# A hybrid decoder step on one core: the fourth gate-and-up tile in seven block products

## The chip, the core and the metric

The kernel runs on one core of a Trainium2 chip. A core has five engines that each work through their own queue in order: TensorE (PE: matmuls, with the weight load beside it, PEld), VectorE (DVE), ScalarE (ACT), GpSimd (POOL) and SyncE (SP), which here only issues transfers. Engines wait for each other by semaphores. Matmul results go to PSUM, which has eight banks; everything else lies in SBUF. The metric is the device time of one execution in microseconds, the median of several runs. The profile shows one further execution.

## The reference

One step of a decoder layer for 520 tokens: 512 of a prompt and 8 samples, which share the weights. Model width 1024. The layer has a recurrent branch and an attention branch, and then the part that the change touches, a SwiGLU feed-forward layer of width 2816:

```python
h2 = rms_norm(x, norm2_g) * (1.0 + sc2) + sh2
gu, up = jnp.split(h2 @ w_ffn_in, 2, axis=-1)
x = x + g2 * ((jax.nn.silu(gu) * up) @ w_ffn_out)
```

All data are float32.

## The kernel before

Activations lie transposed: 128 features on the partitions, 520 tokens along the free axis, worked in two halves of 260 tokens, left (L) and right (R). To keep float32 accuracy with the faster float32r matmul, every operand is split into a high and a low part: ScalarE casts the high part ("whi", "wb", "tuh"), VectorE subtracts it for the low part ("wlo", second half of "wb", "tul"). Every product is three matmuls: high by high, low weight by high, high weight by low.

The feed-forward layer goes over 22 tiles of 128 columns, each with a gate and an up part. Tiles 0 and 1 are done plainly by halves (groups "fi", lines 1654 to 1679), tiles 2 and 3 plainly by `ffn_tile` ("fig" and "fiu", two products of 48 matmuls each): 96 matmuls of 260 tokens for a tile. From tile 4 (`GROUP`) on, `fast_tile` uses a Winograd form of Strassen's scheme. The 2 x 2 blocks are gate and up by the two halves of the 1024 features for the weights (a11, a12, a21, a22), and the halves of features by the halves of tokens for the input. Seven block products of 12 matmuls (four chunks of 128 features, three matmuls each) take the place of eight: 84 matmuls. For them POOL forms four sums of the weights of each tile (s1 to s4, lines 261 to 264, tile "ws"), and once for all tiles the sums u and w of the input (`h2_blocks`, lines 1593 to 1600; each has a left and a right part, for four chunks k). The sums are split into high and low parts by `split_blocks` ("tu" and "tw"). The seven products add up in four banks X, Y, W, Z; VectorE combines these (line 1617), ScalarE takes the silu of the gate, and `close` multiplies and splits a half of the tile's output for the second matrix.

The products with the second matrix ("fo") are strewn between the blocks of later tiles (`JOIN`): the group of tiles 0 to 3 is multiplied during tiles 4 to 7, the first of them after block S2 of tile 4.

Order. `begin` runs before each product: it loads weights that are due within 22 us and splits those due within 11 us, by an estimated length of each unit (5.36 us for a plain product, 1.34 us for a block). `units` lists the products in order. The weight sums of a tile are issued when its first block, A11, is split. Raw weights of a tile have two buffers ("wraw"), split weights three of each of two tags ("whi", "wlo"), and seven buffers of the tag "pg" hold h2 before its split, the weight sums and the second matrix's raw weights. Instructions traced in this order go to a planner, which makes the order on each engine from it: what is ready by its own estimate may go ahead of what is not. `issue_after` holds a block of instructions behind a given one; `split_blocks` stands behind the silu that was traced last. `defer(k, ...)` runs a function after the k-th product from now: the sums of chunks 0 and 1 are split after tile 2's gate product, those of chunks 2 and 3 after its up product.

Of the kernel before, what the change touches and what calls it, by code (L numbers as in the profile page):

```python
# [11 lines left out]
AF = mybir.ActivationFunctionType  # L12
ALU = mybir.AluOpType
# [10 lines left out]
FF = 2816  # L24
# [4 lines left out]
HALF = NT // 2  # L29
# [36 lines left out]
def kernel(ctx, tc, xT, par, gates, b_f, cst, cse, own, cache_k, cache_v, cache_lf, pt,  # L66
# [3 lines left out]
    pe, act, dve, pool, sp = nc.tensor, nc.scalar, nc.vector, nc.gpsimd, nc.sync  # L70
# [46 lines left out]
    def cols(src, c0, n=256, k0=0, nk=KT):  # L117
        return [(src, k0, nk, c0, n)]
# [21 lines left out]
    GROUP = 4  # L140
    PLAIN = 2
    LAST = 16
    JOIN = {}
    for jt in range(GROUP, LAST):
        JOIN[jt] = {"S2": (jt // GROUP - 1, 2 * (jt % GROUP)), "A12": (jt // GROUP - 1, 2 * (jt % GROUP) + 1)}
    for i, (jt, name) in enumerate(((16, "S2"), (16, "A12"), (17, "A12"), (18, "A12"), (19, "A12"), (20, "A12"),
                                    (21, "S2"), (21, "A12"))):
        JOIN.setdefault(jt, {})[name] = (LAST // GROUP - 1, i)
    BLOCKS = ("A11", "S2", "S3", "S1", "A12", "A22", "S4")
    units = []  # L150

    def whole(c):
        for o in range(0, sum(p[4] for p in chunks[c]), 128):
            units.append((c, o, chunks[c][0][2]))
# [4 lines left out]
    for jt in range(FF // 128):  # L159
        c = len(chunks)  # L160
        chunks.append(cols(w_fi, 128 * jt, 128) + cols(w_fi, FF + 128 * jt, 128))
        if jt < GROUP:
            whole(c)
            continue
        for name in BLOCKS:
            units.append((c, name, 4))
            if name in JOIN[jt]:
                g, i = JOIN[jt][name]
                if i % 2 == 0:
                    joined.add(len(chunks))  # L170
                    chunks.append(cols(w_fo, 128 * i, 256, 128 * GROUP * g, GROUP))
                units.append((max(joined), 128 * (i % 2), GROUP))
# [8 lines left out]
    state = {"n": 0, "dma": 0, "split": 0, "load": 22, "lead": 11, "due": 0, "age": 1}  # L181
# [73 lines left out]
    def split_block(raw, name):  # L255
        if name == "A11":
            a11, a12, a21, a22 = (raw[:, k:k + 4, o:o + 128] for o in (0, 128) for k in (0, 4))
            s12, s34 = (pgp.tile([128, 8, 128], F32, name="ws", tag="pg") for _ in range(2))
            s1, s2, s3, s4 = s12[:, :4], s12[:, 4:], s34[:, :4], s34[:, 4:]
            blocks.update(A11=a11, A12=a12, A22=a22, S1=s1, S2=s2, S3=s3, S4=s4)  # L260
            pool.tensor_tensor(s1, a21, a22, ALU.add)  # L261
            pool.tensor_tensor(s2, s1, a11, ALU.subtract)
            pool.tensor_tensor(s3, a11, a21, ALU.subtract)
            pool.tensor_tensor(s4, a12, s2, ALU.subtract)
        return split_four(blocks[name])

    def split_four(src):
        state["tag"] = "wlo" if state.get("tag") == "whi" else "whi"
        t = wp.tile([128, KT, 128], F32R, name="wb", tag=state["tag"], bufs=3)
        state["act"] = act.copy(t[:, :4], src)  # L270
        state["last"] = dve.tensor_tensor(t[:, 4:], src, t[:, :4].bitcast(F32), ALU.subtract)  # L271
        return [t[:, k] for k in range(4)], [t[:, 4 + k] for k in range(4)]
# [9 lines left out]
    def defer(k, fn):  # L282
        later.setdefault(state["n"] + k, []).append(fn)
# [50 lines left out]
    def split(name, raw, scale=None):  # L334
        hi = slot(name + "h", dt=F32R)
        lo = slot(name + "l", dt=F32R)
        if scale is None:
            act.copy(hi, raw)
            dve.tensor_tensor(lo, raw, hi.bitcast(F32), ALU.subtract)
        else:  # L340
            act.activation(hi, raw, AF.Copy, scale=scale)
            dve.scalar_tensor_tensor(lo, raw, scale, hi.bitcast(F32), ALU.mult, ALU.subtract)
        return hi, lo
# [551 lines left out]
    for i in range(KT):  # L895
        if i % 4 == 0:
            qtp.append(bank(f"qt{i}", NS))
        if i < 6:
            t = qpart[i]
            for j, (t0, t1) in enumerate(HALVES):  # L900
                b = bank(f"q{i}_{j}")
# [672 lines left out]
    def pair_out():  # L1574
        return slot("ach", dt=F32R), slot("acl", dt=F32R)

    def ffn_tile(jt):
        t, out = slot("sw"), pair_out()
        product(f"fig{jt}", h2, lambda j, b: swish(b, t, j))

        def up(j, b):
            t0, t1 = HALVES[j]
            times_up(b, t, j)
            split_part(out, t[:, t0:t1], slice(t0, t1))

        product(f"fiu{jt}", h2, up)
        return out


    L_, R_ = slice(0, HALF), slice(HALF, NT)  # L1590
    tb, traw = [], []
# [7 lines left out]
        pool.tensor_tensor(u[:, R_], b2[:, L_], w[:, L_], ALU.subtract)  # L1599
        traw.append((u, w))  # L1600

    def split_blocks(k0):
        with tc.issue_after(state["silu"].ins):
            for k in range(k0, k0 + 2):
                u, w = traw[k]
                tb.append((split("tu", u), split("tw", w)))

    def h2_block(name, k):
        pair, part = {"A11": (h2[k], L_), "A12": (h2[k + 4], L_), "S4": (h2[k + 4], R_), "S1": (tb[k][0], L_),
# [3 lines left out]
    def fast_tile(jt, ac):  # L1613
        sw, cp, u2, out = slot("sw"), slot("cp"), slot("u2", HALF), pair_out()
        X, Y, W, Z = (bank(f"fi{jt}{n}")[:, :HALF] for n in "xywz")
        into = {"A11": X, "S2": Y, "S3": W, "S1": Z, "A12": X, "A22": W, "S4": Z}
        add = lambda o_, a_, b_: dve.tensor_tensor(o_, b_, a_, ALU.add)

        def close(b, part):
            dve.tensor_tensor(b, b, sw[:, part], ALU.mult)  # L1620
            split_part(out, b, part)

        for m_, name in enumerate(BLOCKS):
            n = begin()
            hi, lo = splits[n]
            for k in range(4):
                ah, al = h2_block(name, k)
                for m, (wt, at) in enumerate(((hi, ah), (lo, ah), (hi, al))):
                    state["mm"] = pe.matmul(into[name], lhsT=wt[k], rhs=at, start=m_ < 4 and k == 0 and m == 0,
                                            stop=k == 3 and m == 2, skip_group_check=m_ > 3)  # L1630
            if name == "A11":
                act.copy(cp[:, L_], X)
            elif name == "S2":
                add(u2, cp[:, L_], Y)
            elif name == "S3":
                add(W, u2, W)
            elif name == "S1":
                act.copy(cp[:, R_], Z)  # L1638
                add(Z, u2, Z)
                add(Y, cp[:, R_], W)  # L1640
            elif name == "A12":
                act.activation(sw[:, L_], X, AF.Silu)
            elif name == "A22":
                close(W, L_)
            elif name == "S4":
                act.activation(sw[:, R_], Z, AF.Silu)
                close(Y, R_)
            run_later(n)
            if name in JOIN[jt]:
                g, i = JOIN[jt][name]  # L1650
                product(f"fo{g}_{i}", ac[GROUP * g:GROUP * g + GROUP], lambda j, b_, i=i: residual(i, b_, 5, j))
        return out

    ac, ts, ready = [], [slot("sw") for _ in range(PLAIN)], []
    u = state["n"]
    for j in range(2):
        for m in range(2 * PLAIN):
            if j == 0:
                begin(u + 3)
            b = bank(f"fi{m}_{j}")  # L1660
# [10 lines left out]
            first = u + 2 * PLAIN  # L1671
# [8 lines left out]
    for jt in range(PLAIN, FF // 128):  # L1680
        if jt == PLAIN:
            for k in range(4):
                h2_blocks(k)
            defer(0, lambda: split_blocks(0))
            defer(1, lambda: split_blocks(2))
        ac.append(fast_tile(jt, ac) if jt >= GROUP else ffn_tile(jt))
    last_product(ac[LAST:])


# [60 lines left out]
```

## Time and profile before

| | us |
|---|---|
| median of 3 runs | 1027.86 (1024.04 to 1030.81) |
| profiled execution | 1027.04 |
| its span, first to last instruction | 1025.3 |
| TensorE busy | 994.1 (97%) |
| VectorE busy | 792.7 (77%) |
| ScalarE busy | 553.3 (54%) |
| POOL busy | 331.4 (32%) |

The mean granted clock of TensorE was 0.993 of full speed. In the rows of the profile a line number is that of the code above, then come engine, operation, and output<-inputs by the program's names, with shapes. In a timeline the first two numbers are start and length in us; a bracket gives the idle time of the engine before the instruction and what ended it. In the chain of work a row is start, length, engine and name. A row of the wait table gives who waited for whom: us in total, times, longest.

### The profile page before, as it was taken

To read this page: it belongs to the slowest core of one execution; us is meant where nothing else is said; L and a number is where in the kernel's file an instruction comes from. 1 tells how busy PE (TensorE), PEld (TensorE's weight loads), DVE (VectorE), ACT (ScalarE), POOL (GpSimd) and SP (SyncE) were. 2 spreads that over 40 slices of the span, in tenths; PEclk is the share of its full clock that TensorE was granted. 3 is DMA by queue.
4 is the path that set the end of the run, shared out by engine and by line. 5 is a ranking of instruction groups with operands and counts; after the bars stand their busy time and mean duration, and the time that the engine had idled before them with its cause. 6 is when DMAs were issued, how large, how long until landed. Compare 5 with 4: busy or idle time off the path is not lost.

```text
span 1025.3 us, 21277 instructions
## 1 busy us (share of the span) xinstructions
PE 994.1 (97%) x7994; PEld 921.1 (90%) x7994; DVE 792.7 (77%) x1423; ACT 553.3 (54%) x1132; POOL 331.4 (32%) x424
## 2 busy tenths in 40 slices
PE   4999999999999999999999999999999999999996
PEld 1888989999999988888888989999999999999996
DVE  5446999998999978887656554878888878888764
ACT  4433665857682267777875234464444444445453
POOL 0224511111135135454430001494442433434212
PEclk9899999999999999999999999999999999999999
DMA  9888987778899999997775784324243242333212
GB/s 324 308 278 292 306 284 222 261 232 276 266 277 322 322 324 292 287 311 219 235 236 190 252 295 114 83 63 122 64 124 105 82 124 78 88 104 104 63 63 84
DMA packets 164378, 206.98 MB, mean 202 GB/s; under 512 B 9890, under 2 KB 125106, under 8 KB 164210
## 3 DMA queue, kind: packets, MB, share of 16 engines
q1 hardware_dynamic: 147554, 152.52, 47.7%
q0 software_dynamic: 13040, 46.67, 13.9%
q10 hardware_dynamic: 3680, 6.42, 1.7%
q8 instruction: 63, 1.03, 0.4%
q14 instruction: 41, 0.34, 0.1%
HBM read 192.49 MB, written 13.09 MB: 201 GB/s over the span
## 4 chain that ended last, share of the span: by engine, by line
PE 86%; DVE 6%; DMA 4%; ACT 1%; issue 1%; POOL 1%; SPq 0%; DVEq 0%; ACTq 0%; POOLq 0%
PE fo L305 12%; PE gr L305 5%; PE gb L305 5%; PE pa L305 5%; PE pb L305 4%; PE v L305 4%; PE k L305 4%; PE ga L305 4%; PE xr L305 3%; PE pv L817 3%; PE wo L305 3%; DMA wraw<-in_w_in_dram 2%; PE qp L527 2%; PE po L1273 2%; PE q L527 1%; PE ptt L1239 1%
## 5 line engine op out<-in xcount | busy, mean ns | idle before, releaser
L246 ACT CAST whi<-wraw 128x1024 fp32r<-128x1024 f32 (+1 forms) x79 | 82.0, 1040 | 114.2 <-PE pb L305 35.1
L248 DVE TENSOR_TENSOR wlo<-wraw,whi 128x1024 fp32r<-128x1024 f32 (+1 forms) x79 | 100.4, 1272 | 22.9 <-ACT whi L246 20.1
L270 ACT CAST wb<-ws 128x512 fp32r<-128x512 f32 x72 | 44.7, 621 | 91.0 <-PE fo L305 63.6
L305 PE MATMUL fo<-ach,wb 128*128 128x260 f32 x512 | 93.3, 282 | 0.0
L682 POOL DMA_DIRECT2D pg<-in_cache_k_dram x74 | 39.5, 534 | 143.4 <-DVE S L731 77.0
L271 DVE TENSOR_TENSOR wb<-wraw,wb 128x512 fp32r<-128x512 f32 x86 | 74.3, 864 | 6.5 <-ACT wb L270 5.4
L305 PEld LDWEIGHTS fo<-ach,wb 128*128 128x128 f32 x512 | 78.9, 188 | 0.0
L261 POOL TENSOR_TENSOR ws<-wraw 128x512 f32<-128x512 f32 x18 | 26.1, 1449 | 153.6 <-DMA wraw<-in_w_fi_dram 121.1
L271 DVE TENSOR_TENSOR wb<-ws,wb 128x512 fp32r<-128x512 f32 x72 | 63.1, 876 | 15.3 <-ACT wb L270 13.4
L270 ACT CAST wb<-wraw 128x512 fp32r<-128x512 f32 x86 | 53.5, 622 | 37.7 <-ACT cp L1638 6.5
L305 PE MATMUL fo<-acl,wb 128*128 128x260 f32 x256 | 72.2, 282 | 0.0
L730 DVE TENSOR_TENSOR pg<-pg,qb 128x1024 f32<-128x1024 f32 x48 | 57.9, 1219 | 0.8 <-DMA pg<-in_cache_k_dram 0.8
L731 DVE TENSOR_REDUCE S<-pg 128x16 f32<-128x1024 f32 x48 | 57.4, 1209 | 0.3
L1230 POOL TENSOR_SCALAR p<-p,mu 128x128 f32<-128x128 f32 (+3 forms) x28 | 38.7, 1391 | 52.2 <-DVE mu L1226 38.1
L305 PEld LDWEIGHTS fo<-acl,wb 128*128 128x128 f32 x256 | 48.2, 188 | 0.0
L1224 ACT ACTIVATE p<-p,mu 128x128 f32<-128x128 f32 (+3 forms) x64 | 35.4, 554 | 18.7 <-DVE mu L1223 18.4
L305 PE MATMUL v<-hh,whi 128*128 128x260 f32 x128 | 37.9, 296 | 0.8 <-ACT row L797 0.5
L305 PE MATMUL pb<-oh,whi 128*128 128x260 f32 x128 | 36.8, 287 | 1.0 <-ACT oh L1331 1.0
L305 PE MATMUL k<-hh,whi 128*128 128x260 f32 x128 | 37.3, 291 | 0.0
L305 PE MATMUL gb<-hh,whi 128*128 128x260 f32 x128 | 37.0, 289 | 0.0
L305 PE MATMUL v<-hl,whi 128*128 128x260 f32 x128 | 37.0, 289 | 0.0
L305 PE MATMUL v<-hh,wlo 128*128 128x260 f32 x128 | 36.9, 288 | 0.0
(1099 smaller groups left out, 3968.6 us busy)
## 6 DMA issues: line engine op xcount, KB each, us to landing
araw<-in_ada_w_dram SPq DMA_DIRECT2D x48, 512.0 KB, 6.4
wraw<-in_w_fi_dram SPq DMA_DIRECT2D x44, 512.0 KB, 4.3
pg<-in_cache_k_dram POOLq DMA_DIRECT2D x42, 512.0 KB, 5.8
pg<-in_cache_v_dram SPq DMA_DIRECT2D x42, 512.0 KB, 5.4
wraw<-in_w_in_dram SPq DMA_DIRECT2D x34, 512.0 KB, 7.4
wraw<-in_w_in_dram SPq DMA_DIRECT2D x11, 1024.0 KB, 9.3
pg<-in_cache_v_dram POOLq DMA_DIRECT2D x22, 512.0 KB, 6.2
pg<-in_cache_k_dram POOLq DMA_DIRECT2D x32, 256.0 KB, 5.8
```

The costliest lines, as they stand in the source:

```text
L246: state["act"] = act.copy(hi[:, :k1 - k0], src)
L248: state["last"] = dve.tensor_tensor(lo[:, :k1 - k0], src, hi[:, :k1 - k0].bitcast(F32), ALU.subtract)
L270: state["act"] = act.copy(t[:, :4], src)
L271: state["last"] = dve.tensor_tensor(t[:, 4:], src, t[:, :4].bitcast(F32), ALU.subtract)
L305: state["mm"] = pe.matmul(out[:, :t1 - t0], lhsT=wt[k], rhs=at, start=k == 0 and m == 0, stop=k == nk - 1 and m == 2)
L527: state["mm"] = pe.matmul(b[:, :HALF], lhsT=wt, rhs=at[:, t0:t1], start=k == 0 and m == 0, stop=k == 3 and m == 2)
L682: done.append(eng.dma_start(pg, cache[bass.ds(r, 1), :, c0:c1].rearrange("a p c -> (a p) c")))
L730: dve.tensor_tensor(pg, pg, q, ALU.mult)
L731: last = dve.tensor_reduce(S[r // 2][:, c:c + H], pg.rearrange("p (h d) -> p h d", d=DH), AX.X, ALU.add)
L817: pe.matmul(pv[0][32 * gq:32 * gq + 32, :], lhsT=pw[r][:, c:c + 32], rhs=pgs[gq // 2][:, 512 * hf:512 * hf + 512], start=j == 0, stop=j == ...
L1224: act.activation(p[:, :n + 128], p[:, :n + 128], AF.Exp, bias=mu[:, 0:1], scale=-1.0, accum_out=mu[:, 1:2])
L1230: (pool.tensor_scalar(p, p, mu[:, 2:3], None, ALU.mult) if a and i + 1 < KT else act.activation(p, p, AF.Copy, scale=mu[:, 2:3]))
```

## The change

Tile 3 is computed by `fast_tile` too. Its blocks have an order of their own (A11, A12, S4, S2, S3, S1, A22 instead of A11, S2, S3, S1, A12, A22, S4). As S4 comes before the products that it is added to, it has a bank of its own ("v"), is copied to SBUF and added after S1; the right half of the output is closed after S1, the left half after A22. On POOL the tile's fourth weight sum is traced before the third. The input's sums are split in one go after tile 2's gate product: the four w, then the four u.

```diff
-    BLOCKS = ("A11", "S2", "S3", "S1", "A12", "A22", "S4")
+    BLOCKS = [("A11", "S2", "S3", "S1", "A12", "A22", "S4")] * (FF // 128)
+    FIRST = 3
+    BLOCKS[FIRST] = ("A11", "A12", "S4", "S2", "S3", "S1", "A22")
...
-        if jt < GROUP:
+        if jt < FIRST:
             whole(c)
             continue
-        for name in BLOCKS:
+        for name in BLOCKS[jt]:
...
             pool.tensor_tensor(s1, a21, a22, ALU.add)
             pool.tensor_tensor(s2, s1, a11, ALU.subtract)
+            if "V" not in state:
+                pool.tensor_tensor(s4, a12, s2, ALU.subtract)
             pool.tensor_tensor(s3, a11, a21, ALU.subtract)
-            pool.tensor_tensor(s4, a12, s2, ALU.subtract)
+            if "V" in state:
+                pool.tensor_tensor(s4, a12, s2, ALU.subtract)
+            state["V"] = 1
...
-    def split_blocks(k0):
+    def split_blocks():
         with tc.issue_after(state["silu"].ins):
-            for k in range(k0, k0 + 2):
-                u, w = traw[k]
-                tb.append((split("tu", u), split("tw", w)))
+            tw = [split("tw", w) for _, w in traw]
+            tb.extend(zip([split("tu", u) for u, _ in traw], tw))
...
+        first = jt == FIRST
+        if first:
+            into["S4"] = bank(f"fi{jt}v")[:, :HALF]
+            v = slot("v4", HALF)
...
                 add(Z, u2, Z)
                 add(Y, cp[:, R_], W)
+                if first:
+                    add(Z, v, Z)
+                    act.activation(sw[:, R_], Z, AF.Silu)
+                    close(Y, R_)
             elif name == "A12":
                 act.activation(sw[:, L_], X, AF.Silu)
             elif name == "A22":
                 close(W, L_)
+            elif name == "S4" and first:
+                act.copy(v, into[name])
...
-            defer(0, lambda: split_blocks(0))
-            defer(1, lambda: split_blocks(2))
-        ac.append(fast_tile(jt, ac) if jt >= GROUP else ffn_tile(jt))
+            defer(0, split_blocks)
+        ac.append(fast_tile(jt, ac) if jt >= FIRST else ffn_tile(jt))
```

In the matmuls, `start` is set for the first block in a bank instead of by the block's number.

More of the change, by code (lines that the diff above doesn't have):

```diff
@@ L161 @@
         chunks.append(cols(w_fi, 128 * jt, 128) + cols(w_fi, FF + 128 * jt, 128))
-        if jt < GROUP:
+        if jt < FIRST:
             whole(c)
             continue
-        for name in BLOCKS:
+        for name in BLOCKS[jt]:
             units.append((c, name, 4))
-            if name in JOIN[jt]:
+            if name in JOIN.get(jt, ()):
                 g, i = JOIN[jt][name]
@@ L1616, in fast_tile @@
         into = {"A11": X, "S2": Y, "S3": W, "S1": Z, "A12": X, "A22": W, "S4": Z}
+        first = jt == FIRST
+        if first:
+            into["S4"] = bank(f"fi{jt}v")[:, :HALF]
+            v = slot("v4", HALF)
+        begun = []
         add = lambda o_, a_, b_: dve.tensor_tensor(o_, b_, a_, ALU.add)
@@ L1621, in close @@
             split_part(out, b, part)
-        for m_, name in enumerate(BLOCKS):
+        for name in BLOCKS[jt]:
+            fresh = not any(into[name] is b for b in begun)
+            begun.append(into[name])
             n = begin()
@@ L1628, in fast_tile @@
                 for m, (wt, at) in enumerate(((hi, ah), (lo, ah), (hi, al))):
-                    state["mm"] = pe.matmul(into[name], lhsT=wt[k], rhs=at, start=m_ < 4 and k == 0 and m == 0,
-                                            stop=k == 3 and m == 2, skip_group_check=m_ > 3)
+                    state["mm"] = pe.matmul(into[name], lhsT=wt[k], rhs=at, start=fresh and k == 0 and m == 0,
+                                            stop=k == 3 and m == 2, skip_group_check=not fresh)
             if name == "A11":
@@ L1648, in fast_tile @@
             run_later(n)
-            if name in JOIN[jt]:
+            if name in JOIN.get(jt, ()):
                 g, i = JOIN[jt][name]
```

## The prediction

> **What bounds the kernel now.** I read the page's head first, then the wait table of TensorE for the last part of the span, then the chain of work around the fourth tile (index 3, "tile 3" below).
>
> ```profile
> span 1025.3 us, 21277 instructions
> PE 994.1 (97%) x7994; PEld 921.1 (90%) x7994; DVE 792.7 (77%) x1423; ACT 553.3 (54%) x1132; POOL 331.4 (32%) x424
> PE 86%; DVE 6%; DMA 4%; ACT 1%; issue 1%; POOL 1%; SPq 0%; DVEq 0%; ACTq 0%; POOLq 0%
> ...
> PE r L404 <- DVE ss L397: 1.4, 1, 1.4
> PE fi L305 <- DVE h2l L1474: 1.1, 3, 0.4
> PE r L1552 <- ACT sq L1540: 0.2, 1, 0.2
> ```
>
> TensorE is busy 97% and holds 86% of the chain. The last three rows are all the waits of TensorE from 600 us to the end: 2.7 us in 425. So in the stage of the change TensorE's own work sets the time, and taking work off it counts in full as long as nothing new makes it wait.
>
> ```profile
> 671.65 0.27 POOL h2r L1467
> ...
> 673.58 0.97 DVE h2l L1474
> ...
> 674.59 8.42 PE fi L305 x68
> 683.01 5.75 PE fig L305 x48
> 688.76 5.78 PE fiu L305 x48
> 694.54 5.76 PE fig L305 x48
> 700.30 5.78 PE fiu L305 x48
> 706.09 1.45 PE fi4x L1629 x12
> 707.53 1.44 PE fi4y L1629 x12
> 708.98 2.88 PE fo L305 x24
> 711.85 1.42 PE fi4w L1629 x12
> ...
> 723.38 1.44 PE fi5y L1629 x12
> ```
>
> This is the chain in order of time (start, length, instructions). Tiles 2 and 3 are two products each (gate "fig", up "fiu"), tile 4 is the first in seven blocks. From 674.59 the pieces touch: no gap on TensorE up to 713. Just before, the chain runs over POOL's sample columns of h2 and VectorE's "h2l".
>
> **What the change removes on TensorE.** Tile 3 takes 96 matmuls today (694.54 to 706.09: 5.76 + 5.78 = 11.54 us). Afterwards it takes 7 blocks of 12, 84 matmuls. A block of this shape lasts 1.42 to 1.45 us, so 7 x 1.44 = 10.10 us. The saving is **1.44 us**, 0.14% of the span, and nothing else on TensorE changes. This is the whole upside; the rest of the work is to find what the change may cost in waits.
>
> If TensorE does not wait, tile 3's blocks start at 694.5 (A11), 696.0 (A12), 697.4 (S4), 698.9 (S2), 700.3 (S3), 701.7 (S1) and 703.2 (A22), and tile 4 starts at 704.6 in place of 706.1. Each block needs its weights split by then, and S2, S3, S1, A22 also the input's sums: w by 698.9, u by 701.7.
>
> **What it adds on POOL.** Tile 3 now needs the four weight sums. POOL's rows of today:
>
> ```profile
> 666.60 0.32 POOL L1466 TENSOR_TENSOR h2r<-h2r,n2amp 128x8 f32<-128x8 f32 x1 [9.65 <-DVE h2r L1462]
> ...
> 671.88 0.74 POOL L1596 TENSOR_TENSOR u<-h2r 128x260 f32<-128x260 f32 x1
> ...
> 685.76 0.74 POOL L1598 TENSOR_TENSOR w<-h2r 128x260 f32<-128x260 f32 x1
> 686.46 1.20 POOL L1599 TENSOR_TENSOR u<-h2r,w 128x260 f32<-128x260 f32 x1
> 688.46 1.29 POOL L261 TENSOR_TENSOR ws<-wraw 128x512 f32<-128x512 f32 x1 [0.80 <-DMA wraw<-in_w_fi_dram]
> ...
> 692.80 2.15 POOL L264 TENSOR_TENSOR ws<-wraw,ws 128x512 f32<-128x512 f32 x1
> ```
>
> The sixteen input sums run from 671.88 to 687.66, tile 4's weight sums from 688.46 to 694.95 (6.49 us). The code asks for tile 3's weight sums while the first two tiles finish, before the input sums, so in program order they come at 671.92, behind the sample columns. At the length of tile 4's group, everything behind them moves 6.5 us: input sums end at about 694.2 (the last of w at 686.50 + 6.5 = 693.0), tile 4's sums at about 701.5. One ScalarE cast and one VectorE subtract later (rows below: 0.62 and 0.69 to 1.83 us) the last w is split by 695.5, and TensorE wants its fourth chunk at 698.9 + 9 x 0.12 = 700.0: 4.5 us in hand. The last u is split by about 697 and wanted at 701.7 + 1.1: over 5 us. Tile 4's first summed block is wanted at 704.6 + 1.45 = 706.1 and ready at about 704, since S1 and S2 are the first two of its four sums. Splitting all w ahead of all u serves this order. In time POOL holds.
>
> **What it adds on VectorE and ScalarE.**
>
> ```profile
> 683.42 1.76 DVE L248 TENSOR_TENSOR wlo<-wraw,whi 128x1024 fp32r<-128x1024 f32 x1
> ...
> 689.74 1.83 DVE L339 TENSOR_TENSOR tul<-u,tuh 128x520 fp32r<-128x520 f32 x1 [2.68 <-ACT tuh L338]
> 691.49 2.31 DVE L248 TENSOR_TENSOR wlo<-wraw,whi 128x1024 fp32r<-128x1024 f32 x1
> ...
> 695.77 0.69 DVE L339 TENSOR_TENSOR tul<-u,tuh 128x520 fp32r<-128x520 f32 x1
> ...
> 698.27 0.68 DVE L271 TENSOR_TENSOR wb<-ws,wb 128x512 fp32r<-128x512 f32 x1
> ...
> 713.31 0.44 DVE L1617 TENSOR_TENSOR fi4w<-fi4w,u 128x260 f32<-128x260 f32 x1
> ...
> 686.08 0.38 ACT L1516 ACTIVATE sw<-fig 128x260 f32<-128x260 f32 x1
> ...
> 689.08 0.62 ACT L338 CAST tuh<-u 128x520 fp32r<-128x520 f32 x1
> 689.60 1.05 ACT L246 CAST whi<-wraw 128x1024 fp32r<-128x1024 f32 x1
> ```
> ```profile
> 683.00:694.40 11.40, 11.40 (x98) 11.40 (x97) 8.03 (x7) 4.34 (x8) 10.52 (x8) 1.00 0.48 139
> 694.40:706.00 11.60, 11.60 (x99) 11.60 (x98) 10.43 (x17) 6.00 (x13) 6.58 (x4) 1.00 0.47 136
> ```
>
> The two window rows are length, then busy time of TensorE, weight load, VectorE (DVE), ScalarE (ACT), POOL, then the granted clock: 1.00, so no throttle here. VectorE loses two long splits (1.76 + 2.31 = 4.07 us) and gains seven short ones (7 x 0.69 = 4.83) and five adds (5 x 0.43 = 2.15); the two closing multiplies and splits replace equal ones of today. Net 2.9 us, if the added ones run alone. VectorE's idle time in the two windows is 3.37 + 1.17 = 4.54 us, less the 1.44 us that TensorE gains: 3.1 us. It just fits. ScalarE loses two casts of 1.05 and gains seven of 0.62 and three copies the size of the silu of 0.38, some 3.4 us in windows where it idles 12.7 us: nothing, while that cover stands.
>
> How much can the added POOL work slow VectorE? The same subtract takes 0.69 us at 695.77, while POOL rests, and 1.83 us at 689.74, while POOL adds: 1.14 us more. Four more POOL adds can hold up four subtracts: bounds 0 and 4 x 1.14 = 4.6 us of VectorE time. I take 2 us, nearer the low end, because the first of the four sums fall where VectorE has gaps (it was busy 8.13 of 11 us from 672 to 683):
>
> ```profile
> 672.00:683.00 11.00, 10.30 (x84) 9.88 (x83) 8.13 (x9) 7.34 (x13) 11.00 (x13) 1.00 0.01 2
> ```
>
> The Trainium skill, "SBUF — State Buffer", section "Who interferes with whom", speaks against this change: a VectorE instruction with two SBUF inputs and a GpSimd instruction that reads SBUF hold a shared port in turn, each for its whole length, and the later one fully blocks. The trace agrees in size: the 1.14 us above is close to the 1.29 us of a POOL weight sum. By that rule every POOL sum may cost VectorE its whole length, which is rival 2 below.
>
> Where would a late VectorE show? The splits run well ahead: tile 4's S2 split ends at 698.95 and is used at 707.53, so 2 us more delay there is hidden. The tight place is the output half that closes last, which the first output product reads. Today it is the right half:
>
> ```profile
> 706.12 0.43 DVE L1520 TENSOR_TENSOR sw<-fiu,sw 128x260 f32<-128x260 f32 x1 [0.51 <-PE fiu L305]
> ...
> 708.97 0.42 DVE L1479 TENSOR_TENSOR acl<-sw,ach 128x260 fp32r<-128x260 f32 x1
> ```
>
> From the product's end (706.09) to the split (709.39) go 3.3 us; TensorE needs it in the second half of "fo", at 708.98 + 1.44 + 1.08 = 711.5. Afterwards A22 closes the left half last: the end at 704.64 + 3.3 = 707.9, and it is needed in the first half of "fo", at 704.64 + 2.88 + 1.08 = 708.6. The slack falls from 2.1 to **0.7 us**. An extra VectorE lag of 2 us of which half is worked off by then would leave about 0.4 us of wait. I take a wait of **0.4 us** (bounds: 0, and rival 2).
>
> **Transfers, buffers, waits.** Tile 3's weights come by the same transfers at the same time (next fence). Tile 5's are released today by tile 3's last split at 693.8; afterwards by A22's, which waits for A11's weight buffer (free at 696.0), so they go at about 697 and land near 702. They are wanted at tile 5's sums, used from 723.4 on: hidden by 15 us. S4's and S2's casts wait for the buffers of tile 2's gate product, free at 688.76; behind a waiting cast stand the gate's silu and tile 3's other casts on ScalarE. If the first silu (686.08) waits until then, its bank comes free 2.7 us later, and with eight banks TensorE doesn't need it before S4 at 697.4. Price 0. The bank for S4 alone and its copy cost one copy and one add, counted above.
>
> **Sum.** The profiled execution took 1027.04 us, 1.74 us around its span of 1025.3. 1027.04 - 1.44 + 0.4 = 1026.0. It lay 0.82 us under the median of the three runs (1027.86; 1024.04 to 1030.81), so on that scale I forecast **1026.8 us**.
>
> **Rivals.**
>
> 1. *POOL takes tile 3's weight sums early and holds up the norm.* This one ends slower than before. The order on each engine is made by a planner that takes what is ready. POOL idles 9.65 us before 666.60, and tile 3's weights are there by then:
>
> ```profile
> 657.53 25.82 SPq L210 DMA_DIRECT2D wraw<-in_w_fi_dram  x4
> wraw<-in_w_fi_dram SPq DMA_DIRECT2D x12, 512.0 KB, 4.7
> ```
>
> The first of these four issues go at 657.53; with 0.5 us for the second and 4.7 us to landing the weights are there at about 662.7. Four sums of 6.3 us would then hold POOL until 669.0, 2.4 us past the 666.60 at which the sample columns of h2 can start. Those stand on the chain: POOL to 671.92, then "h2l", then TensorE, which already waits 1.1 us for it. The price is up to 2.4 us: 1027.86 - 1.44 + 2.4 = **1028.8 us**. It decides from the point where the first sum starts after 660.3 (666.6 - 6.3) and before 666.6. For it: the gap is free and the data there. Against it: the sums come later in the code, and the trace shows no POOL work that passed other work by so much.
>
> 2. *VectorE becomes the bound at tile 4.* Every POOL sum blocks a subtract (4.6 us) and nothing is worked off before the first "fo": 4.6 - 0.7 = 3.9 us of wait, 1027.86 - 1.44 + 3.9 = **1030.3 us**. It decides when VectorE enters tile 4 over 0.7 us later than now. For it: 10.43 us busy of 11.6. Against it: the splits' lead, and casts and adds that wait for no port.
>
> 3. *Nothing waits:* the saving comes whole, 1027.86 - 1.44 = **1026.4 us**. If moreover the new order shortens the 1.1 us wait for "h2l", 1025.3 us. That the change doesn't do what it says would need more matmuls than 84; the code issues 7 x 12.
>
> **How the numbers follow.** Forecast with a wait under 1 us, 0.40; rival 3, 0.20; rival 1, 0.22; rival 2 in full or in part, 0.15; something unseen that costs over 5 us, 0.03. The cases lie between 1025.3 and 1030.3, closer together than the three runs of one kernel (6.8 us). A median of runs adds some 2 us to either side of the cases with most weight: the range is **1023.4 to 1031.4 us**. The bound of what a measurement tells from no change is about 1%, 10 us, and every case priced here lies within it: same 0.96, slower 0.03 (the unseen), faster 0.01, since no more than 1.44 us is taken from TensorE.
>
> **What would show it.** In the profile after: "fig" and "fiu" with 48 matmuls less each, seven groups of 12 for tile 3, and "fi4x" starting at about 704.6 (706.09 today); TensorE's wait table from 600 us on with a new row under 1 us behind the first "fo". Rival 1 shows as POOL's L261 before 666 and a wait for h2l above 1.1 us; rival 2 as waits of "fo" for "acl" or of tile 3's and 4's blocks for "wb". I would be wrong if POOL's input sums ended after 697, for then w is late for S2, or if a bank or buffer that I count as free holds TensorE up.

## The result

The changed kernel takes 1029.08 us (median of 22 runs, 1025.18 to 1031.91), the kernel before on the same chip 1026.33 us (22 runs). The ratio is 1.0028, 95% interval 1.0017 to 1.004: **slower by 2.75 us**, with an interval of 1.7 to 4.1 us. I had forecast 1.06 us less than before, so the change went the other way.

To find the place I cut the profiles at three instants of TensorE: the matmul that sums the squares for h2's right half ("r"), the first matmul of tile 2 ("fig"), and the first of tile 5 ("fi5x"). These are the rows of TensorE's timeline (start, length, engine, line, operation, output<-inputs) of the kernel before,

```profile
660.29 0.46 PE L404 MATMUL r<-ss,cs 128*128 128x260 f32 x1 [1.35 <-DVE ss L397]
...
682.84 0.28 PE L305 MATMUL fig<-h2h,whi 128*128 128x260 f32 x1
...
721.77 0.29 PE L1629 MATMUL fi5x<-h2h,wb 128*128 128x260 f32 x1
```

and of the changed kernel:

```profile
658.16 0.46 PE L410 MATMUL r<-ss,cs 128*128 128x260 f32 x1 [1.33 <-DVE ss L403]
...
683.33 0.28 PE L311 MATMUL fig<-h2h,whi 128*128 128x260 f32 x1
...
723.04 0.40 PE L1641 MATMUL fi5x<-h2h,wb 128*128 128x260 f32 x2
```

The first stretch, tiles 0 and 1 with the end of the norm, went from 22.55 to 25.17 us, though tile 3 is not in it. The second, tiles 2 to 4, went from 38.93 to 39.71; with 1.44 us saved and nothing lost it would be 37.49. Together they are 3.4 us longer. The span is only 1.3 us longer (1026.6 against 1025.3), because this execution reached "r" 2.1 us earlier; over all profiles of this study "r" starts anywhere from 655.7 to 663.2 us, so spans of single executions can't be compared, and stretches can. Behind "fi5x" hardly anything changed: from there to the end every profile takes 303.2 to 303.8 us.

Now the waits of TensorE and of its weight load in the changed kernel (who waited for whom: us in total, times, longest):

```profile
PE fi L311 <- DVE h2l L1480: 1.5, 3, 1.0
PE r L410 <- DVE ss L403: 1.3, 1, 1.3
PE fi3x L1641 <- ACT cp L1644: 0.9, 1, 0.9
PE fo L311 <- DVE acl L1485: 0.7, 1, 0.7
PE fi L311 <- ACT h2h L1479: 0.5, 1, 0.5
...
PEld fi3x L1641 <- ACT cp L1644: 1.1, 1, 1.1
PEld fo L311 <- DVE acl L1485: 0.9, 1, 0.9
```

Two waits are new: A12 ("fi3x") for ScalarE's copy of A11's bank, and the first output product ("fo") for the low part of tile 3's output. Counted at the weight load they are 2.0 us, which is nearly all of the 2.2 us that the second stretch lost. The wait for h2 has grown from 1.1 us to 2.0 ("h2l" and "h2h" together), at the weight load from 1.7 to 2.9. The reason stands in POOL's timeline:

```profile
661.61 1.29 POOL L263 TENSOR_TENSOR ws<-wraw 128x512 f32<-128x512 f32 x1 [6.79 <-DMA wraw<-in_w_fi_dram]
662.86 1.29 POOL L267 TENSOR_TENSOR ws<-wraw 128x512 f32<-128x512 f32 x1
664.11 1.48 POOL L264 TENSOR_TENSOR ws<-ws,wraw 128x512 f32<-128x512 f32 x1
665.67 1.36 POOL L266 TENSOR_TENSOR ws<-wraw,ws 128x512 f32<-128x512 f32 x1
666.98 0.39 POOL L1472 TENSOR_TENSOR h2r<-h2r,n2amp 128x8 f32<-128x8 f32 x1
```

Tile 3's four weight sums stand ahead of the sample columns of h2, as rival 1 had it. They delay them, and VectorE's products for h2 beside them stretch too: the same four take 1.46 us in the kernel before (first row) and 3.68 us here (second row).

```profile
666.10 1.46 DVE L1462 TENSOR_TENSOR h2r<-x,r 128x260 f32<-128x260 f32 x4
```
```profile
663.98 3.68 DVE L1468 TENSOR_TENSOR h2r<-x,r 128x260 f32<-128x260 f32 x4
```

In this execution the longer waits for h2 make 1.2 us of the 2.6. The rest is in the clock. In the windows of one microsecond below, TensorE's busy time is the second number and the granted clock the third from the end:

```profile
669.00:670.00 1.00, 0.34 (x3) 0.14 (x2) 0.85 (x3) 1.00 (x4) 0.84 (x5) 1.00 0.00 0
670.00:671.00 1.00, 0.67 (x5) 0.67 (x6) 1.00 (x4) 1.00 (x4) 0.59 (x2) 1.00 0.03 8
671.00:672.00 1.00, 0.74 (x5) 0.44 (x3) 1.00 (x4) 1.00 (x5) 0.85 (x3) 0.60 0.00 0
672.00:673.00 1.00, 0.96 (x4) 0.96 (x5) 0.86 (x2) 1.00 (x4) 0.92 (x3) 0.50 0.00 0
673.00:674.00 1.00, 1.00 (x7) 1.00 (x6) 1.00 (x2) 0.98 (x4) 1.00 (x3) 0.50 0.00 0
674.00:675.00 1.00, 1.00 (x8) 1.00 (x7) 1.00 (x2) 0.99 (x2) 1.00 (x2) 0.69 0.00 0
675.00:676.00 1.00, 1.00 (x10) 0.97 (x9) 0.55 (x3) 0.79 (x2) 1.00 (x2) 1.00 0.00 0
```

After the gaps TensorE ran at half clock for 3.4 us (from 671.2 to 674.6): its matmuls started every 0.22 us instead of every 0.12. The kernel before kept 1.00 throughout this stretch.

For tile 3, a window of 13 us from 34 us after "r" on: the kernel before, then the changed one. VectorE is the third busy time, full to the last hundredth.

```profile
694.29:707.29 13.00, 13.00 (x111) 13.00 (x110) 11.60 (x20) 7.29 (x16) 7.90 (x5) 1.00 0.43 122
```
```profile
692.16:705.16 13.00, 12.09 (x100) 11.87 (x100) 13.00 (x22) 8.39 (x18) 2.83 (x2) 1.00 0.16 46
```

How a full VectorE reaches A12 is seen where ScalarE's queue meets VectorE's (changed kernel, timeline of both):

```profile
695.88 1.30 DVE L345 TENSOR_TENSOR twl<-w,twh 128x520 fp32r<-128x520 f32 x2
697.10 1.30 DVE L345 TENSOR_TENSOR tul<-u,tuh 128x520 fp32r<-128x520 f32 x2
698.32 0.42 DVE L1526 TENSOR_TENSOR sw<-fiu,sw 128x260 f32<-128x260 f32 x1
...
698.77 0.41 ACT L1484 CAST ach<-sw 128x260 fp32r<-128x260 f32 x1 [1.15 <-DVE sw L1526]
699.08 0.61 ACT L276 CAST wb<-ws 128x512 fp32r<-128x512 f32 x1
699.60 0.37 ACT L1644 COPY cp<-fi3x 128x260 f32<-128x260 f32 x1
```

A11's last matmul ended at 696.5. ScalarE could have copied its bank then, but its queue first had the cast of tile 2's output, which waited 1.15 us for a VectorE multiply that stood behind the splits of w and u. A12 adds into the bank of A11 and can't start before the copy.

TensorE did not idle all that time, because it does not run the blocks in the order of the code. The planner had put S4 and ten matmuls of S2 between A11 and A12. It also moved A22 ("fi3w" for the second time) behind S1 and 19 matmuls of tile 4, so that only five matmuls are left between A22 and the first "fo". This is the chain of work there:

```profile
700.02 1.71 PE fi3x L1641 x12
701.73 0.24 PE fi3y L1641 x2
701.97 1.45 PE fi3w L1641 x12
703.42 1.43 PE fi3z L1641 x12
704.86 1.43 PE fi4x L1641 x12
706.29 0.84 PE fi4y L1641 x7
707.13 1.57 PE fi3w L1641 x12
...
711.44 1.70 PE fo L311 x12
```

The left half of the output is closed after A22. Its last subtract ("acl") started on VectorE at 710.97, behind a split of weights that took 1.65 us beside POOL's next weight sums (0.68 without one). This is what "fo" waits for.

### The profile page after: what moved, and what is told of

Its sections match the earlier page's. It is cut to its first block, busy times and chain, and to the rows that moved or that the text cites. A ratio compares the mean times of both kernels' runs of the same rounds, so it can differ in the third digit from the quotient of the medians.

```text
span 1026.6 us, 21279 instructions
## 1 busy us (share of the span) xinstructions
PE 993.7 (97%) x7982; PEld 920.4 (90%) x7982; DVE 800.8 (78%) x1433; ACT 555.7 (54%) x1140; POOL 332.7 (32%) x428
## 4 chain that ended last, share of the span: by engine, by line
PE 88%; DVE 5%; DMA 3%; ACT 1%; issue 1%; POOL 1%; SPq 0%; DVEq 0%; POOLq 0%; ACTq 0%
PE fo L311 12%; PE k L311 5%; PE gr L311 5%; PE gb L311 5%; PE v L311 5%; PE pa L311 5%; PE xr L311 5%; PE pb L311 4%; PE ga L311 4%; PE pv L823 3%; PE wo L311 3%; DMA wraw<-in_w_in_dram 2%; PE qp L533 2%; PE po L1279 2%; PE ptt L1245 2%; PE q L533 1%
## 5 line engine op out<-in xcount | busy, mean ns | idle before, releaser
L250 DVE TENSOR_TENSOR wlo<-wraw,whi 128x1024 fp32r<-128x1024 f32 (+1 forms) x77 | 96.4, 1253 | 22.7 <-ACT whi L248 22.4
L276 ACT CAST wb<-ws 128x512 fp32r<-128x512 f32 x76 | 47.1, 622 | 95.0 <-PE fo L311 64.5
L277 DVE TENSOR_TENSOR wb<-wraw,wb 128x512 fp32r<-128x512 f32 x89 | 79.2, 890 | 5.3 <-ACT wb L276 4.7
L277 DVE TENSOR_TENSOR wb<-ws,wb 128x512 fp32r<-128x512 f32 x76 | 65.6, 864 | 15.5 <-ACT wb L276 13.7
L311 PE MATMUL ga<-hh,wlo 128*128 128x260 f32 x128 | 36.3, 284 | 1.0 <-DVE wlo L250 1.0
```

Source lines behind the costliest of these rows:

```text
L250: state["last"] = dve.tensor_tensor(lo[:, :k1 - k0], src, hi[:, :k1 - k0].bitcast(F32), ALU.subtract)
L311: state["mm"] = pe.matmul(out[:, :t1 - t0], lhsT=wt[k], rhs=at, start=k == 0 and m == 0, stop=k == nk - 1 and m == 2)
```

## The experiments

Each line of the table is one kernel. The stretches are from its profile, cut as above; the last column is the measured ratio to the kernel before, with its 95% interval.

| kernel | first stretch | second | both against before | ratio (interval) |
|---|---|---|---|---|
| before | 22.55 | 38.93 | 0 | 1 |
| changed | 25.17 | 39.71 | +3.40 | 1.0028 (1.0017 to 1.004) |
| changed, again | 24.63 | 39.50 | +2.65 | one run |
| changed, again | 24.54 | 39.59 | +2.65 | one run |
| e1: sums behind the sample columns | 24.18 | 41.42 | +4.12 | 1.007 (1.0045 to 1.0094) |
| e2: before, plus the sums | 25.00 | 38.92 | +2.44 | 1.0024 (1.0004 to 1.0044) |
| e3: casts behind the copy | 24.63 | 39.64 | +2.79 | 1.0025 (1.0009 to 1.0042) |
| e4: e1 and e3 | 25.67 | 39.80 | +3.99 | 1.0045 (1.0026 to 1.0064) |
| e5: sums behind the input sums | 22.58 | 45.30 | +6.40 | 1.0062 (1.0045 to 1.0078) |
| e6: no low parts of w and u | 24.56 | 39.47 | +2.55 | 1.0019 (1.0005 to 1.0034) |
| e7: no weight sums in tile 3 | 22.58 | 39.71 | +0.81 | 1.0032 (1.0014 to 1.005) |
| e8: e6 and e7 | 22.56 | 39.36 | +0.44 | 0.9994 (0.998 to 1.0007) |
| e9: other order of blocks | 24.66 | 41.07 | +4.25 | 1.0035 (1.0018 to 1.0052) |
| e10: e9, two sums early, two later | 22.58 | 40.81 | +1.91 | 1.0035 (1.0019 to 1.005) |
| e11: e6, e7 and e9 | 22.55 | 37.79 | -1.14 | 1.0005 (0.999 to 1.0019) |
| e12: e10, w split early | 22.56 | 42.07 | +3.15 | 1.0041 (1.0022 to 1.0059) |
| e13: e12 in the changed order | 22.58 | 44.50 | +5.60 | 1.0043 (1.0027 to 1.0059) |

Some stretches hold a spell of 3.4 us at half clock: the first ones of the changed kernel's first profile, e2 and e4, and the second ones of e5, e9 and e12 (in e13 6.8 us). All other stretches ran at full clock.

### e1 to e4: where do the weight sums stand, and does the copy matter?

e1, the four sums held behind the last sample column:

```diff
-                pool.tensor_tensor(t[:, NP:], t[:, NP:], b_[:, 1:9], ALU.add)
+                state["cols"] = pool.tensor_tensor(t[:, NP:], t[:, NP:], b_[:, 1:9], ALU.add)
...
+            with nullcontext() if "V" in state else tc.issue_after(state["cols"].ins):
+                pool.tensor_tensor(s1, a21, a22, ALU.add)
...
```

> Theory N (the norm): the changed kernel loses most of its time before tile 3, because POOL takes tile 3's four weight sums ahead of the sample columns of h2; TensorE then waits for h2 and runs at half clock for about 3 us afterwards. Here the four sums are held behind the last sample column, all else is the changed kernel. N expects the span from the start of the two plain tiles to tile 2 to be as in the kernel before (2.6 us shorter than in the changed kernel), no window with a granted clock of 0.5, and a time about 2.6 us under the changed kernel's 1029.1: 1026.5. Theory T (the tile): the loss sits in tiles 3 and 4, where VectorE is too busy; sums that come 5 us later make w late, so T expects no gain or a loss, 1029 to 1031.

Theory N was wrong: this profile has no half clock (e4, with the sums at the same place, has one), but the kernel became slower still, +4.1 us by its stretches. Theory T had the direction, not the size. The waits of e1, and POOL's and VectorE's timeline, say why:

```profile
PE fi3x L1642 <- ACT cp L1645: 2.9, 1, 2.9
PE fi L312 <- DVE h2l L1481: 2.7, 3, 1.5
```
```profile
671.16 1.29 POOL L264 TENSOR_TENSOR ws<-wraw 128x512 f32<-128x512 f32 x1
672.41 1.31 POOL L268 TENSOR_TENSOR ws<-wraw 128x512 f32<-128x512 f32 x1
673.68 1.46 POOL L265 TENSOR_TENSOR ws<-ws,wraw 128x512 f32<-128x512 f32 x1
...
672.52 2.90 DVE L1481 TENSOR_TENSOR h2l<-h2r,h2h 128x260 fp32r<-128x260 f32 x2
```

Behind the sample columns the sums fall on VectorE's subtracts for h2: two of them take 2.90 us. The same two take 1.85 in the kernel before, beside input sums, and two with no POOL sum beside them 0.77. So the place is bad on either side of the sample columns. The input sums start 17.0 us after "r" here, 14.2 in the changed kernel, and the wait for the copy grew from 0.9 to 2.9 us.

e2, the kernel before with the same four sums, which nothing reads:

```diff
                 split_upto(first + m - 1)
+                if m == 3:
...
+                    pool.tensor_tensor(s12[:, :4], a21, a22, ALU.add)
+                    pool.tensor_tensor(s12[:, 4:], s12[:, :4], a11, ALU.subtract)
+                    pool.tensor_tensor(s34[:, 4:], a12, s12[:, 4:], ALU.subtract)
+                    pool.tensor_tensor(s34[:, :4], a11, a21, ALU.subtract)
```

> The kernel before, plus four sums of tile 3's raw weights on POOL at the place where the changed kernel traces them; nothing reads them, and tile 3 stays two plain products. Theory N: slower than before by 2.6 us (1026.3 to about 1028.9), with the waits for h2 and the half clock of the changed kernel. Theory T: no difference beyond 0.5 us, since tiles 3 and 4 are as before.

Theory N's number: the sums alone, in a kernel that is otherwise the one before, lengthen the first stretch by 2.45 us, with 1.7 us of waits for h2 and a half clock of their own (its windows of 2 us):

```profile
674.00:676.00 2.00, 1.22 (x8) 1.02 (x8) 2.00 (x7) 2.00 (x8) 1.75 (x6) 1.00 0.02 4
676.00:678.00 2.00, 1.98 (x9) 1.98 (x10) 1.82 (x3) 1.98 (x6) 1.92 (x5) 0.52 0.00 0
```

e3, the casts of tile 2's output held behind the copy of A11's bank, and e4, both edits:

```diff
-            split_part(out, t[:, t0:t1], slice(t0, t1))
+            defer(j, lambda: split_after(out, t[:, t0:t1], slice(t0, t1)))
+
+        def split_after(*a):
+            with tc.issue_after(state["cp"].ins):
+                split_part(*a)
```

> The changed kernel, with ScalarE's casts of tile 2's output held behind the copy of A11's bank, so that A12, which adds into the same bank, need not wait for that copy. Both theories expect the wait of 0.9 us for the copy to go. Theory N: about 1.1 us faster than the changed kernel (1028.0), the wait for h2 and the half clock stay. Theory T: with this wait gone most of the loss of 2.75 us goes, 1026.5 to 1027.

> Both edits at once: the four sums behind the sample columns, the casts behind the copy. Theory N with the copy's wait as a second, separate loss: 2.6 + 1.1 us under the changed kernel, 1025.4, which is 0.9 us faster than the kernel before; what is left of the 1.44 us saving is eaten by the wait at the first output product. Theory T: not faster than the copy edit alone.

In e3 the wait for the copy is gone as expected, and nothing is gained: 0.9 us of it came back as a wait of A22 for VectorE's add after S1, "fi3w" for "fi3y". In e4 that wait is 1.3 us, and e4 is no faster than e3, against theory N. The copy was one place where TensorE met VectorE's queue; the next took over.

### e5 to e8: take the work away

e5 holds the sums behind the last input sum; for that, the weight split of tile 3's first block is traced later too. e6 leaves out the eight subtracts for the low parts of w and u, e7 the four weight sums (raw blocks take their place), e8 both.

```diff
+                return hi, hi
+            tw = [high("tw", w) for _, w in traw]
+            tb.extend(zip([high("tu", u) for u, _ in traw], tw))
...
+            if "V" not in state:
+                blocks.update(S1=a21, S2=a22, S3=a21, S4=a12)
```

> From the first plain product after the norm to tile 2's gate product the kernel before takes 22.55 us, the changed one 25.17; from there to tile 5 38.93 and 39.71, where 84 matmuls in tile 3 would give 37.49. Here tile 3's four sums stand behind the last of the sixteen input sums. Theory O (order alone: what costs is that the sums stand in front of work that is waited for): first stretch back to 22.6, second 39.7, time 1026.5. Theory P (POOL's sums and VectorE's subtracts shut each other out, so the sums cost VectorE some 5 us wherever it is busy): first stretch 22.6, second 41 or more, because the sums now fall among the splits of w and u; time 1028 or more.

> The changed kernel without the eight subtracts that make the low parts of w and u: the products take the high part in both places, so the output is only as exact as that; the matmuls are as many as before. If VectorE's backlog is what makes tiles 3 and 4 wait (for the copy of A11's bank, for the adds, for the split before the first output product), the second stretch falls from 39.7 to 37.5 to 38.2 and the first stays at 24.6 to 25.2: time 1027. If those waits come from the order on ScalarE alone, the second stretch stays at 39.7 and the time at 1029.

> The changed kernel without tile 3's four weight sums: its blocks S1 to S4 take raw blocks in their place, so tile 3's output is another; all else stays. Both theories: first stretch 22.6, no half clock. The time is then 2.6 us under the changed kernel (1026.5) if the second stretch stays at 39.7, as theory O has it; theory P expects the second stretch to shorten too only if the sums fell into it, which they do not in the changed kernel, so 39.7 as well.

> Both left out: the four sums of tile 3 and the eight low parts of w and u. If these two are all that ate the saving, the stretches are 22.6 and 37.5 and the time is 1.44 us under the kernel before: 1024.5. If something else of the change costs time (the bank for S4, the order of blocks), the second stretch stays above 38.5.

e5 went theory P's way and beyond: the first stretch is the old one, the second 45.3 us, with waits of 2.4 us for the copy, 1.4 for w's low part and 1.1 at "fo", and with a half clock again (0.87 in the mean of tile 3's 13 us). The later split of the first block may have a part in it; no run takes the two apart. e7 isolates the norm: without the sums the first stretch is 22.58 us, and the second keeps its 39.71. Its measured time did not follow the forecast of 1026.5 (see the end of this section). e6 was a miss: VectorE's busy time in tile 3 falls from 13.00 to 7.55 us of 13, the wait for the copy goes, but the second stretch falls only to 39.47. In e8 it stays at 39.36, with VectorE busy 9.55 of 13 us. Waits of 0.5 us for the add after S1 and 0.6 us at "fo" remain there although VectorE is not full. In both, A22 still stands five matmuls ahead of "fo", and the subtract that "fo" waits for stands behind a weight split that takes 1.6 us beside POOL's sums.

### e9 to e13: banks or VectorE?

e9 changes the order of tile 3's blocks in the code, so that other blocks stand between A11 and A12, and one between S1 and A22. What TensorE runs differs less: between S1 and A22 stand 19 matmuls as in the changed kernel (now A12 and seven of tile 4), but A12 comes after S1, and between A22 and the first "fo" stand 17 in place of five. e10 takes two weight sums early and two behind the eighth input sum.

```diff
-    BLOCKS[FIRST] = ("A11", "A12", "S4", "S2", "S3", "S1", "A22")
+    BLOCKS[FIRST] = ("A11", "S4", "S2", "S3", "S1", "A12", "A22")
...
+        if k == 1:
+            with tc.issue_after(last.ins):
+                state["rest"]()
```

> The changed kernel with tile 3's blocks in the order A11, S4, S2, S3, S1, A12, A22. In the changed order A12 adds into the bank that A11 has just filled and A22 into the bank that VectorE still has to read after S1, with no block between. Theory B (banks: those two reads are on TensorE's path because nothing covers them): the waits for the copy and for the add go, the second stretch falls from 39.7 to 38.0 to 38.5, the first stays at 24.6 to 25.2 and the time falls to about 1027.7. Theory V (VectorE is too full in tile 3, whatever waits for it): the second stretch stays at 39.3 or more, the wait turns up at the split before the first output product or at the weights, and the time stays at 1029.

> As the order edit, and of tile 3's four weight sums only the first two stand ahead of the sample columns, the other two behind the eighth input sum. Two sums end about 2.5 us after the weights land, before the norm needs POOL: first stretch 22.6 to 23.2 with no wait for h2 beyond 1.1 us (all four ahead of it: 24.6 to 25.7; behind the sample columns 24.2). Second stretch as with the order edit alone under theory B, 38.0 to 38.5, or up to 1 us more since the later sums meet VectorE's splits. Time 1026 to 1027: as the kernel before, at best 0.5 us under it.

With VectorE as full as before, the order alone gains nothing: the waits for the copy and at "fo" go, and one for the add after S1 is now 1.8 us, with a half clock behind it. That is theory V, though it looked for the wait elsewhere. S1 was done at 702.1 in e9, and VectorE reached the first of the adds that follow it at 705.43 (first row), behind splits of weights, the low part of tile 2's output and two other adds. No run moves this add ahead of the splits, so whether VectorE's load or only the order in its queue costs the time here stays open:

```profile
705.43 0.42 DVE L1627 TENSOR_TENSOR fi3z<-fi3z,u 128x260 f32<-128x260 f32 x1
```

e10's first stretch is the old one, 22.58 us: two sums fit before the norm needs POOL (they end at 661.97, the sample columns start at 662.69), which settles the first stretch. Its second has this:

```profile
PE fi3w L1648 <- DVE fi3y L1634: 2.4, 1, 2.4
PE fi L315 <- DVE h2l L1484: 1.1, 3, 0.4
PE fi3z L1648 <- DVE wb L281: 0.5, 1, 0.5
```

Two more profiles of the changed kernel:

> The changed kernel as it is. The half clock after the waits for h2 was there in three of five profiles with the sums early, and absent in two. If it hangs on where the waits fall in time, this profile shows either a first stretch of about 24.6 us and a clock of 1.00, or about 25.2 and a clock of 0.5 for some 3 us; the other waits repeat within 0.2 us.

> The same once more: first stretch 24.6 us at full clock or about 25.2 with some 3 us at half clock; second stretch 39.6 to 39.8.

Both show full clock and 24.6 us: the half clock comes in some executions. Without it the two stretches add up to 2.65 us more than before, with it to 3.40; the measured difference of the medians is 2.75.

Last, both kinds of work left out in the other order, and two complete kernels that split w earlier (e12 with the other order, e13 with the changed one):

```diff
         with tc.issue_after(state["silu"].ins):
-            tw = [split("tw", w) for _, w in traw]
...
+            tw.extend(split("tw", w) for _, w in traw)
```

> The order edit (A11, S4, S2, S3, S1, A12, A22), without tile 3's four weight sums and without the low parts of w and u. The order edit alone had moved the wait for the add after S1 from 0.7 to 1.8 us, leaving out the two kinds of work alone had left waits of 0.5 us for that add and 0.6 us for the split before the first output product. If a full VectorE and the reuse of a bank are both needed for the waits in tile 3, neither is left here: first stretch 22.6, second 37.5 to 37.8, 1.2 to 1.4 us under the kernel before. If the second stretch stays at 39.4, something that I have not named takes the 1.9 us.

> A complete kernel: the order edit, two weight sums early and two behind the eighth input sum, and the split of w no longer held behind tile 2's silu, so that four of the eight subtracts can go to VectorE's gaps before tile 3. If the crowd on VectorE within tile 3 is the cause, the wait for the add after S1 falls from 2.4 us to under 1 and the second stretch to 38 to 39; with a first stretch of 22.6 that is up to 0.9 us under the kernel before. If VectorE and POOL are full together already before tile 3, the subtracts only move the other splits and the second stretch stays at 40.8.

> The same with the changed kernel's own order of blocks (A11, A12, S4, S2, S3, S1, A22). If the crowd on VectorE is the cause, the wait for the copy of A11's bank (0.9 us) goes too and the second stretch is 38 to 39; if the order on the banks decides, it keeps that wait and the one after S1 and stays at 39.5.

In e11 the waits of tile 3 are gone. Its waits from 600 us to the end are those of the kernel before, and the second stretch is 37.79 us, 0.3 over the ideal:

```profile
PE r L414 <- DVE ss L407: 1.3, 1, 1.3
PE fi L315 <- DVE h2l L1484: 1.1, 3, 0.4
PE r L1562 <- ACT sq L1550: 0.2, 1, 0.2
```

e8 and e11 differ only in the order of the blocks. With the changed order and a full VectorE the second stretch is 39.50 to 39.71 us, with the changed order and the work left out 39.36 (e8), with the other order and a full VectorE 41.07 (e9, some of it half clock), with the other order and the work left out 37.79. So neither edit alone brings the stretch down, and both together do. VectorE need not be idle for that: in the same 13 us it is busy 10.55 us in e11 and 9.55 in e8. Which part of the new order brings the add after S1 in time isn't shown, as A22 stands 19 matmuls behind S1 in both.

e12 and e13 missed. Beside POOL's input sums and tile 4's weight sums the subtracts of w take 1.24 to 1.78 us each in e12, where 0.69 is the length alone, and the waits stay (1.8 us for the add in e12, 2.7 us for the copy in e13), with half clocks behind them. No complete kernel of this study beats the kernel before.

Measured times and stretches don't agree everywhere. e7 (3.3 us against 0.81), e1 (7.2 against 4.1) and e11 (0.5 against -1.14, with an interval of -1.0 to +1.9) lie just outside their intervals, e10 on the edge, and all of them on the slow side; the gain of e11 is seen in its stretches alone. One profile of each can't tell whether other executions of these had a half clock or lost time ahead of "r"; this stays open.

## Why the prediction was wrong

- **The saving** was right: 84 matmuls in place of 96, and in e11, where nothing is in the way, 38.93 - 37.79 = 1.14 of the 1.44 us show.
- **"So in program order they come at 671.92, behind the sample columns."** This step failed. The planner took the sums at 661.61, when the weights landed, ahead of the sample columns. Rival 1 had the mechanism with a price of up to 2.4 us and a chance of 0.22; it cost 2.0 us in the two profiles at full clock, and 2.6 us where the clock halved. e2 shows it alone (2.45 us, half clock included), and e7 and e10 take it away. It should have been the forecast: the idle row of POOL and the landing time were both on the page, and the only evidence against it was that the trace showed no such case. The mechanism was the one I had priced there: POOL's sample columns start 8.8 us after "r" (666.98 - 658.16), 2.5 us later than before, for a priced 2.4. The landing itself came 3.45 us after "r", where I had 2.4. What I had not seen is the second half of it: the sums also stretch VectorE's work, whose four products beside them took 2.2 us longer.
- **"In time POOL holds"** was a step for the order that did not come. e1 shows it wrong as well: with the sums where I had put them, h2's subtracts and the copy wait, +4.1 us.
- **"If TensorE does not wait, tile 3's blocks start at ..."** The order was not that one: the planner ran A11, S4, most of S2, A12, the rest of S2, S3, S1, 19 matmuls of tile 4 and then A22. The list of what each block needs was incomplete too: A12 needs A11's bank copied, A22 needs the add that reads its bank after S1. I priced both at nothing without naming them; my sign "if a bank or buffer that I count as free holds TensorE up" came true. Measured at the weight load: 1.1 us at the copy in the changed kernel, 1.1 to 1.6 us at the add once the copy was out of the way (e3, e4).
- **"It just fits"** for VectorE: it did not. VectorE was busy 13.00 of 13 us in tile 3. But in this order of blocks its load alone is not what costs: e6 takes 5.45 us of it away and the second stretch gains at most 0.2 us. In the other order the same work and the sums together cost 3.3 us (e9 against e11, some of it half clock).
- **The wait at the first "fo"**, 0.4 us: right in place, 0.9 us in size at the weight load (0.5 to 0.7 us at the matmul in three profiles). The mechanism was not the lag of a full VectorE that I had: I had counted two whole blocks between A22 and "fo", the planner left five matmuls, and the wait stays at 0.8 to 0.9 us when VectorE's load is taken away (e6, e8). In e11, with 17 matmuls between, it is 0.2. So rival 2, with VectorE as the bound, came true only in that VectorE was full, one tile earlier than I had it.
- The three together: -1.44 + 2.0 (norm) + 2.1 (tile 3 and "fo") = 2.7 us, against a forecast of -1.44 + 0.4.
- Two agreements are luck. Rival 1's 1028.8 us lies close to the measured 1029.08, but it holds the full saving, no loss in tile 3, and a kernel before of 1027.86 where the comparison gave 1026.33. And "fi4x" stands at 704.86 in the chain, near the forecast 704.6, but in an execution that reached "r" 2.1 us earlier, and with A22 still to come.

## What to carry to other kernels

Where an order is made by readiness, work that becomes free of its inputs early will be placed early: look for the first idle gap after its data land, and price what it displaces and whom it shuts out there, before pricing the place where the code asks for it. When blocks are reordered, write down for each block not only what it reads but who must have read its bank, and read from the trace in which order the engine ran them: here the planner, not the list in the code, set how many matmuls stood between. A saving of 1.4 us on an engine that is 97% busy was lost here, where the engine that feeds it was already at 11.6 of 13; taking work off that engine alone did not bring it back, and neither did the order alone.

## What the runs showed of the hardware

TensorE's clock fell to half without an idle spell: in the changed kernel it was busy 0.34 to 0.78 us of each microsecond from 668 to 672 with no gap longer than 1.0 us, and then had a granted clock of 0.5 for 3.4 us. The spells in e2, e4, e5, e9 and e12 have the same length, and e13's is twice as long. The Trainium skill, "TensorE: Matmul & The Clock Gate", section "What's actually happening", has the throttle set in after an idle window of about 3.4 us that runs freely; here no such window was idle, only thinly used. A later section of the page, "A second HAM failure mode: psum-queue depth-cycling", has the clock swing where TensorE idles briefly but often between groups of matmuls; that fits this trace better, though the page names no share of busy time at which it sets in. That much the same waits gave a half clock in some profiles (the changed kernel's first, e2, e4) and not in others (its two repeats, e1, e3) fits a window whose phase is left to chance; no run here tests that. The price was 0.6 us on the changed kernel's first stretch, and 1.5 us between e4 and e1, whose sums stand at the same place (25.67 against 24.18).

That POOL's sums stretch VectorE's two-input instructions I had expected from one pair of durations; the sizes I had not: four products from 1.46 to 3.68 us, two subtracts from 0.77 to 2.90.
